# 64x64 score tiles and another order of steps in the attention stage of a two-layer trunk

## Chip, cores and metric

The kernel runs on one core of a Trainium2 chip. The metric is the device time of one execution in microseconds (us). Before the change the median of 3 runs is 2286.52 us (2284.51 to 2287.61).

## The reference

The program computes two residual layers of width 1024 over 1024 tokens in float32, and a final norm. The even layer mixes with retention and RWKV-7 heads, the odd layer with sliding-window attention, and a SwiGLU feed-forward net (FFN) follows each. The change lies in the attention of the odd layer: 16 query heads of 64 columns in 4 groups, one key and one value head to a group, a window of 128 tokens, and a learned sink value for each head that enters the softmax's maximum and its denominator.

```python
z = h @ w_qkv + b_qkv
q, k, v = jnp.split(z, [SWA_WIDTH, SWA_WIDTH + SWA_KV_HEADS * HEAD_DIM], axis=-1)
...
kb, vb = with_prev(k), with_prev(v)          # the block's own 128 keys, and the 128 before them
s = jnp.einsum('bnqhgd,bnkhd->bnhgqk', q, kb).astype(jnp.float32) * HEAD_DIM ** -0.5
...
band = (rel >= 0) & (rel < W)
...
m = jnp.maximum(jnp.max(s, axis=-1, keepdims=True), sink)
e = jnp.exp(s - m)
p = e / (jnp.sum(e, axis=-1, keepdims=True) + jnp.exp(sink - m))
o = jnp.einsum('bnhgqk,bnkhd->bnqhgd', p.astype(vb.dtype), vb)
return o.reshape(B, T, SWA_WIDTH) @ w_o + b_o
```

Each query sees 128 keys: from its own block those up to itself, and from the block before it the rest. So a square of 128 queries by 128 places holds all its scores: at each place stands either the own key or the previous block's key of the same number.

## The kernel before

**Halves and pairs.** The tokens are cut into two halves (hf 0 and 1) of 512. The attention stage works on 16 pairs, numbered 0 to 15: a pair is one half, one key group g and two neighbouring blocks of 128 queries, with the 4 heads of the group, so 8 squares of 128 by 128. Pairs 0 to 7 belong to half 0. Pairs 0, 2, 4 and 6 begin with the first block of the sequence, which has no block before it (k0 in the code).

**Four steps for each pair**, named by letters in ATTN_PLAN. S(j), `scores` and `block`: TensorE multiplies queries by keys into two PSUM tiles for each block (lines L1703; tags r and c for the pair's first block, m twice for the second). For each of the two heads i, there are two matmuls, e=1 and e=0, which stand in the two halves of TensorE's rows, since a head has 64 columns to contract over; each takes 128 queries and 256 keys (the form 64*128 64x256 in the trace). ScalarE copies the previous block's scores into the square s (L1712), VectorE overwrites it with the own scores where a constant mask allows (L1713). VectorE takes the maximum (L1728, L1729) and the sink term (L1730), ScalarE makes 8 exponentials with sums (L1733), VectorE and GpSimd multiply by the reciprocal (L1734, L1735, L1737), VectorE transposes 32 by 32 blocks into sq (L1743), and SyncE's queue sends sq to a DRAM tile pd. D(j), `fetch`: four DMAs on SyncE's queue bring pd back, rearranged, as pc (L1750). M(j), `sides`: VectorE multiplies pc by a mask (L1757), which keeps the own block's weights, and VectorE and GpSimd subtract the product from pc, each for 4 heads (L1760), which leaves those of the previous block; both are in pT. O(j), `out`: TensorE multiplies pT by the values into the PSUM tile y (L1773), ScalarE makes the high half of the result (L1779) and VectorE the low half (L1780), in the tile n that the output projection reads. Tile s has 1 buffer, sq 1, pc 2, pT 1; s and pc have 4 KB in each partition.

**Filling.** Between these steps ATTN_PLAN puts steps of other generators, a letter for one step: q and k project queries, keys and values of half 1 (function `proj`: 24 matmuls of 512 columns into a PSUM tile f at L1298, L1300 and L1301, then VectorE L1634 and ScalarE L1635), r is a norm, w is the output projection (w_o: `gemm`, L445, L447, L448), p and f are feed-forward work. In `kv` each of the two value projections is followed at once by four transposes on TensorE (L1665) of the projected tile nq into a PSUM tile m, and a ScalarE copy into vt. Weights are loaded by SyncE's queue (L400) into wr and split into a high part (ScalarE, L430) and a low part (VectorE or GpSimd, L431).

**What sets the order.** Each engine takes its instructions in one fixed order, and each wait holds up all behind it. A scheduler puts the instructions of VectorE, ScalarE, GpSimd and SyncE in order; ATTN_PLAN sets in which order they are handed to it, and `behind` ties one instruction behind another on the same engine. TensorE's order is written out in ATTN_ORDER, which `queue` applies: each entry a:n names PSUM tiles, numbered as they first appear, and takes n matmuls from them in turn. PSUM has three tiles f, two m, and one each of r, c and y.

Of the kernel before, what the change touches and what calls it, by code (L numbers as in the profile page):

```python
# [16 lines left out]
P = 128  # L17
# [35 lines left out]
def make_consts():  # L53
    c = np.zeros((P, NCO), np.float32)

    def put(name, v):
        o, w = CO[name]
        c[: v.shape[0], o : o + w] = v.reshape(v.shape[0], w)
# [39 lines left out]
    put("amask", np.concatenate([own, own.T], axis=1))  # L98
# [37 lines left out]
S0 qqq S1 qqq D0 S2 M0 qqk D1 S3 O0 M1 kkk D2 S4 O1 M2 kkk D3 S5 O2 M3 krr D4 S6 O3 M4 rrr D5 S7 O4 M5 rrr D6  # L136
S8 O5 M6 rr D7 S9 O6 M7 D8 S10 O7 M8 D9 wwwwwwww S11 D10 rr f rrrr S12 O8 M9 D11 p S13 O9 M10 D12 pp S14 O10 M11 D13 p
S15 O11 M12 D14 pp O12 M13 D15 p O13 M14 p O14 M15 p O15 p
"""
ATTN_ORDER = """  # L140
# [113 lines left out]
class Kern:  # L254
# [1355 lines left out]
    def attn_open(self, ap):  # L1610
        nc = self.nc
        m = self.const(ap, "amask").rearrange("p (m o t) -> p m o t", m=2, o=1)
        self.own = m[:, 0].to_broadcast([P, 2, P]).bitcast(mybir.dt.uint32)
# [23 lines left out]
    def kv(self, hf, nr, ap):  # L1637
# [20 lines left out]
        if hf:  # L1658
            G.tensor_copy(vt[:, 0, :], pvt[:, 4, :])
        for i in range(2):  # L1660
            vc = self.t(self.pp, [P, HT], "nq", 4)
            yield from self.proj(nr, 10 + i, vc, bias=self.col("bqkv", 10 + i))
            pt = self.pst("m", [P, 4, P])
# [15 lines left out]
    def attn(self, ap, outs, fill, plan):  # L1679
# [7 lines left out]
        ds, pcs, pTs, n8 = {}, {}, {}, {}  # L1687

        def block(hf, g, b, tags, s):
# [8 lines left out]
            pss = [self.pst(tags[e], [P, 2, 256]) for e in range(2)]  # L1698
# [10 lines left out]
            for e in range(2):  # L1709
                o = s.rearrange("p (i e) k -> p e i k", e=2)[:, e]  # L1710
                if not k0:
                    S.copy(o, pss[e][:, :, :P])  # L1712
# [346 lines left out]
```

## Time and profile before

| what | value |
|---|---|
| median of 3 runs | 2286.52 us |
| the profiled execution, its own time | 2286.15 us |
| span in its profile | 2284.4 us |
| instructions | 35190 |
| busy: PE, DVE, ACT, POOL | 2232.7, 1683.9, 1010.9, 1027.2 us |
| attention stage, by the trace | 1363 to 1650 us |

The columns and names: PE is TensorE, DVE VectorE, ACT ScalarE, POOL GpSimd, SP SyncE; a queue of an engine that issues DMAs has a q behind its name. In a list of the timeline each row has the start in us, the duration in us, the engine, the line in the code, the operation, output and inputs by the program's names, shapes, a count of merged instructions, and in brackets how long the engine had stood idle just before and what released it. In the table of stretches the columns are the stretch, its length, the busy time of each engine with its count of instructions, and PEclk, the clock that was granted to TensorE as a share of the full one. In the list of waits each row has an engine, its line and what it waited for, the sum in us, how often, and the longest wait. A busy TensorE is one that has matmuls in progress, not one at its peak.

### The profile page before, as it was taken

How to read it: one execution, taken by the hardware profiler on the slowest of the kernel's cores; microseconds unless marked ns; L12 is line 12 of the kernel's file. 1: busy time of each engine (PE TensorE's matmuls, PEld its weight loads, DVE VectorE, ACT ScalarE, POOL GpSimd, SP SyncE). 2: the span in 40 equal slices, each digit the busy share in tenths (PEclk: the TensorE clock that was granted, in tenths of full speed). 3: DMA queues.
4: the chain of work that ended last, by engine and by line, in shares of the span. 5: the costliest groups of instructions: out<-in, count | busy, mean ns of one | idle time of the engine just before them, and what ended most of it. 6: DMA issues, size and time to landing. Idle time of an engine off the chain costs nothing. (4 is left out here: it accounts for less than half of the span.)

```text
span 2284.4 us, 35190 instructions
## 1 busy us (share of the span) xinstructions
PE 2232.7 (98%) x12816; PEld 1789.4 (78%) x12816; DVE 1683.9 (74%) x2476; ACT 1010.9 (44%) x1906; POOL 1027.2 (45%) x800
## 2 busy tenths in 40 slices
PE   8999999999999999999999998999999999999998
PEld 6777777778878888888888886677688888888886
DVE  7877965876567368887895967877547788888866
ACT  5454544434445333333343465546444333343335
POOL 3122221212341167777777501214303677777675
PEclk9999999999999999999999999999999999999999
DMA  8566554444356456556766334444436466557663
GB/s 276 195 211 207 194 160 131 141 126 129 134 190 221 162 177 214 203 203 221 266 224 242 109 120 135 135 139 160 158 138 228 173 213 214 211 202 283 228 221 116
DMA packets 181853, 423.17 MB, mean 185 GB/s; under 512 B 44464, under 2 KB 55344, under 8 KB 181680
## 3 DMA queue, kind: packets, MB, share of 16 engines
q1 hardware_dynamic: 178272, 414.37, 53.0%
q10 hardware_dynamic: 2832, 4.45, 0.5%
q8 instruction: 102, 1.67, 0.3%
q0 software_dynamic: 576, 2.10, 0.2%
q14 instruction: 71, 0.58, 0.1%
HBM read 283.87 MB, written 131.60 MB: 182 GB/s over the span
## 5 line engine op out<-in xcount | busy, mean ns | idle before, releaser
L289 PE MATMUL ps_f<-n,w 128*128 128x512 f32 x1440 | 358.7, 403 | 8.6 <-ACT w L430 5.9
L289 PEld LDWEIGHTS ps_f<-n,w 128*128 128x128 f32 x1440 | 266.9, 189 | 83.2 <-issue 12.6
L431 POOL TENSOR_TENSOR w<-wr,w 128x512 fp32r<-128x512 f32 x63 | 87.8, 1401 | 296.4 <-ACT w L430 285.5
L430 ACT CAST w<-wr 128x512 fp32r<-128x512 f32 x231 | 140.6, 617 | 150.7 <-PE ps_f L448 50.3
L431 DVE TENSOR_TENSOR w<-wr,w 128x512 fp32r<-128x512 f32 x168 | 126.3, 755 | 61.9 <-ACT w L430 61.5
L1298 PE MATMUL ps_f<-n,w 128*128 128x512 f32 x415 | 166.4, 401 | 4.7 <-ACT u L1464 4.4
L1300 PE MATMUL ps_f<-n,w 128*128 128x512 f32 x415 | 163.7, 395 | 1.2 <-DVE n L462 1.2
L1301 PE MATMUL ps_f<-n,w 128*128 128x512 f32 x415 | 163.8, 395 | 0.0
L431 POOL TENSOR_TENSOR w<-wq,w 128x512 fp32r<-128x512 f32 x91 | 130.8, 1449 | 30.6 <-ACT w L430 30.6
L1298 PE MATMUL ps_m<-n,w 128*128 128x512 f32 x333 | 130.4, 392 | 0.0
L1300 PE MATMUL ps_m<-n,w 128*128 128x512 f32 x333 | 129.6, 389 | 0.0
L1301 PE MATMUL ps_m<-n,w 128*128 128x512 f32 x333 | 129.5, 389 | 0.0
L1308 DVE TENSOR_TENSOR nq<-ps_m,u 128x512 f32<-128x512 f32 x88 | 58.9, 684 | 93.9 <-PE ps_m L1301 93.9
L462 POOL TENSOR_TENSOR n<-nq,n 128x512 fp32r<-128x512 f32 x60 | 100.0, 1678 | 7.6 <-ACT n L460 7.6
L1493 POOL TENSOR_TENSOR w<-wd,w 128x512 fp32r<-128x512 f32 (+1 forms) x62 | 87.5, 1421 | 32.9 <-ACT w L1492 32.7
L1298 PEld LDWEIGHTS ps_f<-n,w 128*128 128x128 f32 x415 | 78.9, 190 | 27.6 <-ACT u L1464 5.2
L1300 PEld LDWEIGHTS ps_f<-n,w 128*128 128x128 f32 x415 | 78.9, 190 | 18.6 <-DVE n L462 1.6
L1301 PEld LDWEIGHTS ps_f<-n,w 128*128 128x128 f32 x415 | 78.7, 190 | 17.4 <-issue 0.7
L1298 PE MATMUL ps_m<-cb,w 128*128 128x512 f32 x236 | 91.9, 389 | 0.3 <-DVE nq L1308 0.3
L1300 PE MATMUL ps_m<-cb,w 128*128 128x512 f32 x236 | 91.8, 389 | 0.0
L1301 PE MATMUL ps_m<-cb,w 128*128 128x512 f32 x236 | 91.8, 389 | 0.0
L1493 POOL TENSOR_TENSOR w<-ws,w 128x512 fp32r<-128x512 f32 (+1 forms) x48 | 71.8, 1500 | 44.3 <-ACT w L1492 39.0
(533 smaller groups left out, 6355.8 us busy)
## 6 DMA issues: line engine op xcount, KB each, us to landing
hc<-n SPq DMA_DIRECT2D x84, 512.0 KB, 3.3
wsp<-w SPq DMA_DIRECT2D x54, 512.0 KB, 3.5
w<-wsp SPq DMA_DIRECT2D x54, 512.0 KB, 3.4
n<-hc SPq DMA_DIRECT2D x54, 512.0 KB, 6.7
wq<-in_w_gate SPq DMA_DIRECT2D x44, 512.0 KB, 4.4
u<-u SPq DMA_DIRECT2D x88, 256.0 KB, 3.2
ha<-hc SPq DMA_DIRECT2D x34, 512.0 KB, 5.6
hid<-n SPq DMA_DIRECT2D x66, 256.0 KB, 2.0
```

Of the source, the lines that this page charges most:

```text
L289: i = self.nc.tensor.matmul(out, lhsT, rhs, **kw)
L430: nc.scalar.copy(hi[:, :n], raw[:, c])
L431: self.lo.tensor_tensor(out=lo[:, :n], in0=raw[:, c], in1=hi.bitcast(F32)[:, :n], op=ALU.subtract)
L462: e.tensor_tensor(out=lo, in0=src, in1=hi.bitcast(F32), op=ALU.subtract)
L1298: i = mm(ps, hi, xh, start=first and k == 0, stop=False, skip_group_check=True)
L1300: mm(ps, hi, xl, start=False, stop=False, skip_group_check=True)
L1301: mm(ps, lo, xh, start=False, stop=last and k == len(w) - 1, skip_group_check=True)
L1308: self.last_add = V.tensor_tensor(out=o, in0=x, in1=y, op=ALU.add)
L1493: nc.gpsimd.tensor_tensor(out=lo, in0=v, in1=hi.bitcast(F32), op=ALU.subtract)
```

## The change

It has these parts.

1. Scores. A block's scores for one pair of heads come from 64x64 tiles of TensorE in place of two 64x128 ones: queries 0 to 63 take 192 keys (the previous block's 128 and the own block's first 64); queries 64 to 127 take the own block's 128 keys and the previous block's last 64, in two matmuls. For each i there are six matmuls, in the order 192 keys (e=1, e=0), 128 keys (e=1, e=0), 64 keys (e=1, e=0), in place of two; in the first block of the sequence there are four. The PSUM tile has 192 columns for each i in place of 256: columns 64 to 127 of the upper queries hold the previous block's keys, columns 0 to 63 and 128 to 191 the own ones. The mask for own keys is restricted to the query's own half of 64, and the overwriting (now L1732) reads the third group of 64 columns for both halves; in the first block ScalarE copies 64 columns for the upper 64 queries, 8 copies more in all.
2. s has 2 buffers, pc has 1.
3. The multiplication by the mask of M(j) (now L1779) stands behind the sink term's addition of S(j+2) (now L1752) on VectorE.
4. In `kv` both value projections come first, then the transposes (now L1670). In ATTN_PLAN the letters k are 10 in place of 8, and D(j) comes right after M(j-1).
5. ATTN_ORDER is written for the new tiles: the transposes of half 1 stand behind O5 and O6, and a third group of 18 output-projection matmuls stands ahead of O7.

```diff
--- before.py
+++ after.py
@@ -95,7 +95,8 @@
         g2[64:, p] = gm[2 * p + 1]
     put("gam", g2)
     own = np.tri(P, dtype=np.float32)
-    put("amask", np.concatenate([own, own.T], axis=1))
+    x = np.arange(P) // 64
+    put("amask", np.concatenate([np.where(x[:, None] == x[None, :], own, 0.0), own.T], axis=1))
     put("eps", np.tile(np.array([[RMS_EPS, RET_EPS, RWKV_EPS, math.log(0.5)]], np.float32), (P, 1)))
     return c
 
@@ -133,19 +134,19 @@
 
 
 ATTN_PLAN = """
-S0 qqq S1 qqq D0 S2 M0 qqk D1 S3 O0 M1 kkk D2 S4 O1 M2 kkk D3 S5 O2 M3 krr D4 S6 O3 M4 rrr D5 S7 O4 M5 rrr D6
-S8 O5 M6 rr D7 S9 O6 M7 D8 S10 O7 M8 D9 wwwwwwww S11 D10 rr f rrrr S12 O8 M9 D11 p S13 O9 M10 D12 pp S14 O10 M11 D13 p
-S15 O11 M12 D14 pp O12 M13 D15 p O13 M14 p O14 M15 p O15 p
+S0 qqq S1 qqq D0 S2 M0 D1 qqk S3 O0 M1 D2 kkk S4 O1 M2 D3 kkk S5 O2 M3 D4 krr S6 O3 M4 D5 rrr S7 O4 M5 D6 rrr
+S8 O5 M6 D7 krr S9 O6 M7 D8 k S10 O7 M8 D9 wwwwwwww S11 rr f rrrr S12 O8 M9 D10 p S13 O9 M10 D11 pp S14 O10 M11 D12 p
+S15 O11 M12 D13 pp O12 M13 D14 p O13 M14 D15 p O14 M15 p O15 p
 """
 ATTN_ORDER = """
-1:24 2:16 0:1 2:8 3:24 5:24 7:2 4:4 7:22 8:2 6:4 8:22 9:24 10:24 11:1 12,13:4 14,15:4 16:24 17:12 18,19:4 20,21:4
...
+1:24 2:16 0:1 2:8 3:24 4:24 7:22 5:4 7:2 8:2 6:4 8:22 9:24 10:24 11:1 12,13:8 14,15:12 16:24 17:12 18,19:12 20,21:12
...
 """
 
 
@@ -1610,7 +1611,7 @@
     def attn_open(self, ap):
         nc = self.nc
         m = self.const(ap, "amask").rearrange("p (m o t) -> p m o t", m=2, o=1)
-        self.own = m[:, 0].to_broadcast([P, 2, P]).bitcast(mybir.dt.uint32)
+        self.own = m[:, 0].rearrange("p o (x t) -> p o x t", x=2).to_broadcast([P, 2, 2, 64]).bitcast(mybir.dt.uint32)
         self.key = m[:, 1].rearrange("p o (q t) -> p q o t", q=4).to_broadcast([P, 4, 8, 32])
         self.sink = self.t(ap, [P, 16], "sink")
         nc.scalar.dma_start(self.sink, self.A["sinks"].to_broadcast([P, 16]))
@@ -1657,9 +1658,13 @@
             yield
         if hf:
             G.tensor_copy(vt[:, 0, :], pvt[:, 4, :])
+        vcs = []
         for i in range(2):
             vc = self.t(self.pp, [P, HT], "nq", 4)
             yield from self.proj(nr, 10 + i, vc, bias=self.col("bqkv", 10 + i))
+            vcs.append(vc)
+            yield
+        for i, vc in enumerate(vcs):
             pt = self.pst("m", [P, 4, P])
             for b in range(4):
                 nc.tensor.transpose(pt[:, b, :], vc[:, P * b : P * b + P], self.cst["ident"])
@@ -1684,7 +1689,7 @@
         mm = nc.tensor.matmul
         pairs = [(hf, g, b) for hf in range(2) for g in range(4) for b in (0, 2)]
         n = len(pairs)
-        ds, pcs, pTs, n8 = {}, {}, {}, {}
+        ds, pcs, pTs, n8, sinks = {}, {}, {}, {}, {}
 
         def block(hf, g, b, tags, s):
 
@@ -1695,26 +1700,43 @@
             k0 = int(hf == 0 and b == 0)
             k1 = P * b + P
             kp = k1 - P * (1 - k0)
-            pss = [self.pst(tags[e], [P, 2, 256]) for e in range(2)]
+            pss = [self.pst(tags[e], [P, 2, 192]) for e in range(2)]
+
+
             for i in range(2):
-                for e in (1, 0):
-                    a = slice(64 * e, 64 * e + 64)
-                    src = (kc if e == rg else ks)[ti]
-                    mm(
-                        pss[e][:, i, P * k0 :], qt[2 * g + i][a, P * b : P * b + P], src[a, kp : k1 + P],
-                        start=True, stop=True,
-                    )
+                parts = [(0, slice(kp, kp + 192), slice(0, 192))]
+                if k0:
+                    parts = [(0, slice(k1, k1 + 64), slice(P, 192))]
+                parts.insert(1, (1, slice(k1, k1 + P), None))
+                if not k0:
+                    parts.append((1, slice(kp + 64, kp + P), slice(64, P)))
+                for x, kk, c in parts:
+                    for e in (1, 0):
+                        a = slice(64 * e, 64 * e + 64)
+                        po = pss[e][64 * x : 64 * x + 64, i]
+                        r = (kc if e == rg else ks)[ti][a, kk]
+                        mm(
+                            po[:, c] if c else po.rearrange("p (y t) -> p y t", t=64)[:, 0:3:2],
+                            qt[2 * g + i][a, P * b + 64 * x : P * b + 64 * x + 64],
+                            r if c else r.rearrange("p (y t) -> p y t", t=64), start=True, stop=True,
+                            skip_group_check=True,
+                        )
             if k0:
                 G.memset(s, -1e30)
             for e in range(2):
                 o = s.rearrange("p (i e) k -> p e i k", e=2)[:, e]
-                if not k0:
+                if k0:
+                    S.copy(o[64:, :, :64], pss[e][64:, :, :64])
+                else:
                     S.copy(o, pss[e][:, :, :P])
-                V.copy_predicated(o, self.own, pss[e][:, :, P:])
+                V.copy_predicated(
+                    o.rearrange("p i (x t) -> p i x t", x=2), self.own,
+                    pss[e][:, :, P:].rearrange("p i (o t) -> p i o t", o=1).to_broadcast([P, 2, 2, 64]),
+                )
 
         def scores(j):
             hf, g, b0 = pairs[j]
-            s = self.t(ap, [P, 2, 4, P], "s", 1)
+            s = self.t(ap, [P, 2, 4, P], "s", 2)
             for i in range(2):
                 block(hf, g, b0 + i, ("rc", "mm")[i], s[:, i])
             s8 = s.rearrange("p b h k -> p (b h) k")
@@ -1727,7 +1749,7 @@
             m2, es2 = (t.rearrange("p (b h) -> p b h", b=2) for t in (m, es))
             V.tensor_reduce(out=m, in_=s8, axis=AX.X, op=ALU.max, negate=True)
             V.tensor_tensor(out=m2, in0=m2, in1=heads(self.nsink), op=ALU.min)
-            V.tensor_tensor(out=es2, in0=m2, in1=heads(self.sink), op=ALU.add)
+            sinks[j] = V.tensor_tensor(out=es2, in0=m2, in1=heads(self.sink), op=ALU.add)
             S.activation(es, es, AF.Exp)
             for h in range(8):
                 S.activation(s8[:, h], s8[:, h], AF.Exp, bias=m[:, h : h + 1], accum_out=den[:, h : h + 1])
@@ -1745,7 +1767,7 @@
             nc.sync.dma_start(d.rearrange("q t k x -> (q t) (k x)"), sq.rearrange("p k h t -> p (k h t)"))
 
         def fetch(j):
-            pc = pcs[j] = self.t(ap, [P, 4, 8, 32], "pc", 2)
+            pc = pcs[j] = self.t(ap, [P, 4, 8, 32], "pc", 1)
             for k in range(4):
                 nc.sync.dma_start(
                     pc[32 * k : 32 * k + 32].rearrange("p q h t -> p q (h t)"), ds[j][:, :, k].rearrange("q t x -> t q x")
@@ -1754,7 +1776,9 @@
         def sides(j):
             pc = pcs[j]
             pT = pTs[j] = self.t(ap, [P, 2, 4, 8, 32], "pT", 1)
-            V.tensor_tensor(out=pT[:, 1], in0=pc, in1=self.key, op=ALU.mult)
+            x = V.tensor_tensor(out=pT[:, 1], in0=pc, in1=self.key, op=ALU.mult)
+            if j + 2 in sinks:
+                self.behind(x, sinks[j + 2])
             for i, e in enumerate((V, G)):
                 h = slice(4 * i, 4 * i + 4)
                 e.tensor_tensor(out=pT[:, 0, :, h], in0=pc[:, :, h], in1=pT[:, 1, :, h], op=ALU.subtract)
```

Three places in the engines' orders. First VectorE, in the softmax of pair 4 (st holds its maxima, s its square; pT and pc belong to pair 2; n and ps_y to the output of pair 1; nq is a value projection). Before:

```order
L1728 TENSOR_REDUCE st_13202<-s_13182 128x8
L1757 TENSOR_TENSOR pT_13234<-pc_13177,c_amask_12331 128x1024
L1780 TENSOR_TENSOR n_2020_13102<-ps_y_13223,n_2016_13098 128x2x2x128
L1729 TENSOR_TENSOR st_13202<-st_13202,nsink_12335 128x8
L1760 TENSOR_TENSOR pT_13234<-pc_13177,pT_13234 128x4x128
L1730 TENSOR_TENSOR st_13202<-st_13202,sink_12333 128x8
L431 TENSOR_TENSOR w_13482<-wr_13480,w_13482 128x512
L1634 TENSOR_TENSOR nq_13239<-ps_f_13248,rs_12721 128x512
L1734 TENSOR_TENSOR st_13202<-st_13202 128x8
```

The same place of the changed kernel:

```order
L1750 TENSOR_REDUCE st_13276<-s_13242 128x8
L1751 TENSOR_TENSOR st_13276<-st_13276,nsink_12335 128x8
L1804 TENSOR_TENSOR n_2020_13162<-ps_y_13297,n_2016_13158 128x2x2x128
L1752 TENSOR_TENSOR st_13276<-st_13276,sink_12333 128x8
L1779 TENSOR_TENSOR pT_13308<-pc_13179,c_amask_12331 128x1024
L1784 TENSOR_TENSOR pT_13308<-pc_13179,pT_13308 128x4x128
L1756 TENSOR_TENSOR st_13276<-st_13276 128x8
```

The multiplication by the mask and the subtraction moved from between the maximum and the sink term to behind the sink term; the output's low half (L1780, now L1804) moved behind the first of the two small operations on the maxima, and the value projection moved out of this piece.

Second TensorE, at the transposes of the first value projection of half 1 (ps_f is a projection's PSUM tile, L1665 the four transposes, L1703 the scores of pair 5). Before:

```order
L1298 MATMUL ps_f_13290<-n_1944_12698,wx_13284 128x512
L1300 MATMUL ps_f_13290<-n_1948_12702,wx_13284 128x512
L1301 MATMUL ps_f_13290<-n_1944_12698,wx_13284 128x512
L1665 MATMUL ps_m_13275<-c_ident_154,nq_13239 128x128 x4
L1703 MATMUL ps_c_13310<-ks_1913_12469,q_1969_12795 128x256
L1703 MATMUL ps_r_13309<-kc_1908_12433,q_1969_12795 128x256
```

In the changed kernel the first transposes stand here, behind scores with their new tiles (L1718) and an output step (L1797):

```order
L1718 MATMUL ps_m_13778<-ks_2027_13198,q_2064_13466 64x2x64
L1718 MATMUL ps_m_13777<-kc_2004_13078,q_2064_13466 64x2x64
L1718 MATMUL ps_m_13778<-ks_2027_13198,q_2064_13466 64x64
L1718 MATMUL ps_m_13777<-kc_2004_13078,q_2064_13466 64x64
L1797 MATMUL ps_y_13816<-pT_13700,vt_12393 64x256 x8
L1670 MATMUL ps_m_13836<-c_ident_154,nq_13318 128x128 x4
L1299 MATMUL ps_f_13851<-n_1943_12697,w_13845 128x512
```

They moved from a place half a projection behind the one that they read, ahead of pair 5's scores, to one behind the output of pair 5.

Third TensorE, at the output of pair 7, the last of half 0 (n holds what the output projection reads; ps_f tiles are the output projection's). Before:

```order
L447 MATMUL ps_f_13912<-n_2022_13104,w_13909 128x512
L448 MATMUL ps_f_13912<-n_2018_13100,w_13909 128x512
L1773 MATMUL ps_y_13850<-pT_13799,vt_12393 64x256 x8
L1703 MATMUL ps_c_13810<-kc_2003_13029,q_2065_13383 128x256
L1703 MATMUL ps_r_13809<-ks_2026_13133,q_2065_13383 128x256
```

And in the changed kernel, where ps_f_14114 is the third output tile:

```order
L446 MATMUL ps_f_14114<-n_2018_13160,wx_14111 128x512
L448 MATMUL ps_f_14114<-n_2022_13164,wx_14111 128x512
L449 MATMUL ps_f_14114<-n_2018_13160,wx_14111 128x512
L1797 MATMUL ps_y_14018<-pT_13945,vt_12393 64x256 x8
L1718 MATMUL ps_c_13962<-kc_2004_13078,q_2064_13466 64x192
L1718 MATMUL ps_r_13961<-ks_2027_13198,q_2064_13466 64x192
```

In both orders the output of pair 7 is followed by the scores of pair 10, and those by the output projection's matmuls that read pair 7's result (6 for each tile held back). Two tiles stood ahead of it before and three now, 18 matmuls more.

14 rows, old and new, of the table ATTN_ORDER are left out of this document.

## Prediction

> **What bounds the kernel now.** I read the page first, then the stretches of the attention stage, then TensorE's waits in it, then the timelines around the longest waits.
>
> ```profile
> span 2284.4 us, 35190 instructions
> PE 2232.7 (98%) x12816; PEld 1789.4 (78%) x12816; DVE 1683.9 (74%) x2476; ACT 1010.9 (44%) x1906; POOL 1027.2 (45%) x800
> ```
>
> TensorE is busy for all but 51.7 us of the span. So only two things can shorten the program: TensorE standing idle less, and TensorE's work taking less time. The stretches of the attention stage, in the first three rows, show how much of either lies where the change is. The last four rows are short stretches in which the granted clock is half.
>
> ```profile
> 1363.00:1485.00 122.00, 108.24 (x581) 81.30 (x581) 94.61 (x157) 69.25 (x234) 22.71 (x18) 0.96 0.39 131
> 1485.00:1550.00 65.00, 60.39 (x272) 47.43 (x271) 45.88 (x76) 31.44 (x94) 11.05 (x8) 0.95 0.39 130
> 1550.00:1650.00 100.00, 93.28 (x476) 68.81 (x476) 63.64 (x93) 58.15 (x149) 41.05 (x29) 0.97 0.51 169
> 1425.30:1432.10 6.80, 3.05 (x14) 2.38 (x16) 5.20 (x8) 4.79 (x19) 1.46 (x1) 0.50 0.07 18
> 1442.40:1445.80 3.40, 3.16 (x10) 2.68 (x11) 3.39 (x4) 1.28 (x3) 1.58 (x2) 0.50 0.20 59
> 1500.40:1507.20 6.80, 5.65 (x13) 4.46 (x14) 6.10 (x11) 3.00 (x7) 1.27 (x1) 0.50 0.45 159
> 1609.60:1616.40 6.80, 5.60 (x13) 4.44 (x14) 4.95 (x10) 4.58 (x17) 4.21 (x3) 0.50 0.61 213
> ```
>
> TensorE is idle for 122 - 108.24 = 13.76 us, 65 - 60.39 = 4.61 us and 100 - 93.28 = 6.72 us: 25.1 us, half of the idle time of the whole span in an eighth of it. It also works 3.05 + 3.16 + 5.65 + 5.60 = 17.46 us at half clock, where the full clock would need half of that: another 8.7 us. Each of these stretches begins in or ends a long wait; here are TensorE's waits, with the sum, the count and the longest.
>
> ```profile
> PE ps_m L1665 <- ACT nq L1635: 10.3, 2, 7.8
> PE ps_f L1298 <- ACT u L1464: 4.8, 2, 4.4
> PE ps_f L447 <- DVE n L1780: 2.9, 1, 2.9
> PE ps_c L1703 <- DVE s L1713: 2.0, 1, 2.0
> PE ps_f L445 <- ACT n L1779: 1.8, 1, 1.8
> PE ps_y L1773 <- DVE pT L1760: 1.1, 3, 0.6
> PE ps_y L1773 <- DVE n L1780: 0.9, 1, 0.9
> ```
>
> The largest is the two transposes of half 1's values, which stand right behind the projections that they read, while VectorE and ScalarE evict these in turn behind a softmax. The output projection waits for pair 7's result (1.8 + 2.9). The others are a feed-forward wait (4.4), a score tile that is not yet free (2.0), and small ones.
>
> **The change part by part.**
>
> *Transposes of V.* They no longer stand ahead of pair 5's scores but behind outputs 5 and 6, a whole pair of work later, and the wait for L1635 (10.3) goes, with the half clock behind it: (3.05 + 3.16)/2 = 3.1. I keep 1 of it for a PSUM tile m that is now taken among scores. [...] In the trace the second of these waits lasted 10.3 - 7.8 = 2.5 us, and the clock stood at 0.50 for the 3.4 us from 1442.4 on, so a wait of 2.5 is priced with a half-clock stretch. [...]
>
> *The output of pair 7.* 18 more output-projection matmuls stand ahead of it. At a spacing of 0.23 us (the first two rows below) that is 4.1 us in which ScalarE gets through pair 9's exponentials, which stood in front of L1779. Waits of 1.8 + 2.9 and clock of 5.65/2 = 2.8 make 7.5; 0.5 stays.
>
> ```profile
> 1492.02 0.39 PE L447 MATMUL ps_f<-n,w 128*128 128x512 f32 x1
> 1492.25 0.39 PE L448 MATMUL ps_f<-n,w 128*128 128x512 f32 x1
> 1492.57 1.95 PE L1773 MATMUL ps_y<-pT,vt 128*64 128x256 f32 x16
> ```
>
> *Two buffers for s.* ScalarE's copies into s wait for the transpose out of the same buffer, and everything behind them on ScalarE waits too, u of the feed-forward net (L1464, 4.4) among it.
>
> ```profile
> ACT s L1712 <- DVE sq L1743: 23.4, 9, 4.6
> DVE st L1734 <- ACT s L1733: 12.3, 6, 2.5
> ```
>
> (The second row is VectorE's, for the first stretch alone, and is used below.) With a second buffer the first row's wait goes, so the score tiles come free earlier (2.0 of TensorE) and u is not held: 4.4 with its clock 5.60/2 = 2.8, of which I keep 1.0. VectorE's own order of copies is the same, so its part of the chain does not get shorter by this.
>
> *Masks later.* Between the maximum and the exponentials VectorE does other work, and then stands idle while ScalarE makes them:
>
> ```profile
> 1406.79 1.22 DVE L1728 TENSOR_REDUCE st<-s 128x8 f32<-128x1024 f32 x1
> 1407.93 1.22 DVE L1757 TENSOR_TENSOR pT<-pc,c_amask 128x1024 f32<-128x1024 f32 x1
> ...
> 1410.43 0.68 DVE L1760 TENSOR_TENSOR pT<-pc,pT 128x512 f32<-128x512 f32 x1
> ...
> 1413.86 0.17 DVE L1734 TENSOR_TENSOR st<-st 128x8 f32<-128x8 f32 x1 [2.07 <-ACT s L1733]
> 1414.91 1.53 DVE L431 TENSOR_TENSOR w<-wr,w 128x512 fp32r<-128x512 f32 x1
> 1420.77 1.22 DVE L1728 TENSOR_REDUCE st<-s 128x8 f32<-128x1024 f32 x1
> ```
>
> From one maximum to the next this chain took 1420.77 - 1406.79 = 13.98 us. L1757 (1.22) leaves the stretch ahead of the exponentials, and it and L1760 (0.68) now lie in the wait of 2.07, so the chain falls by 1.9 to 12.1 us. TensorE needs for a pair 36 projection matmuls (36 x 0.23 = 8.3), an output (1.95, the row above) and scores (1.93 before, 1.5 after, below): 11.7. The two are near each other. This pair's chain holds a split (L431) of 1.53 us, and without such a one TensorE leads; I allow the difference, 0.4 us, as a new wait in each of the eight pairs beside projections: 3.2. The two kinds of waits of L1773 (1.1 + 0.9) I let stay, since pT now comes later against its scores.
>
> *One buffer for pc.* Its next fetch starts after pair j's subtractions. The loop is the mask, GpSimd's subtraction, four issues on SyncE's queue (the median in ns is the middle number of the first row) and the landing (the last number of the third):
>
> ```profile
> L1750 SPq DMA_DIRECT2D pc<-pd x64: 303/428/507, 1382.0 to 1626.9; - x64
> L1760 POOL TENSOR_TENSOR pT<-pc,pT 128x512 f32<-128x512 f32 x16 | 21.5, 1345 | 73.6 <-DVE pT L1757 47.0 <-DVE st L1729 19.2 <-issue 5.4
> pc<-pd SPq DMA_DIRECT2D x64, 128.0 KB, 3.0
> SPq L400 <- DVE w L431: 52.7, 12, 8.1
> ```
>
> 1.2 + 1.35 + 4 x 0.43 + 3.0 = 7.3 us, below the 11.7 of a pair: I cost it at nothing, hidden behind TensorE's projections. The last row, waits of weight loads on that queue, is used in a rival below.
>
> *Scores.* One group of scores, and the output behind it, before; rows of the same group are left out:
>
> ```profile
> 1395.67 0.45 PE L1703 MATMUL ps_c<-kc,q 64*128 64x256 f32 x1 [1.98 <-DVE s L1713]
> 1395.68 0.48 PE L1703 MATMUL ps_r<-ks,q 64*128 64x256 f32 x1
> 1395.96 0.38 PE L1703 MATMUL ps_c<-kc,q 64*128 64x256 f32 x1
> ...
> 1396.18 0.38 PE L1703 MATMUL ps_c<-kc,q 64*128 64x256 f32 x1
> ...
> 1397.60 0.65 PE L1773 MATMUL ps_y<-pT,vt 128*64 128x256 f32 x4
> ```
>
> 16 rows in 1397.60 - 1395.67 = 1.93 us. A matmul leaves two rows (two passes of 256 columns), rows of the two tiles overlap, and one tile's passes come every 0.21 to 0.22 us (1395.96, 1396.18): 0.43 for each block and i. The new form does not occur in the trace; the nearest rows are 64x64 tiles elsewhere, and one form in two orders:
>
> ```profile
> 325.59 1.96 PE L289 MATMUL ps_m<-GG 64*64 64x128 f32 x32
> 80.18 1.15 PE L289 MATMUL ps_m<-c_ident,AR 64*64 64x64 f32 x32
> 225.36 1.71 PE L289 MATMUL ps_m<-AR,BK 64*128 64x128 f32 x16
> 534.74 1.17 PE L289 MATMUL ps_m<-AR,BK 64*128 64x128 f32 x16
> ```
>
> By the first two, two tiles at a time, a pass takes 1.96/16 = 0.12 us at 128 columns and 1.15/16 = 0.07 at 64, start and end of the burst included; by columns, 0.22/2 = 0.11 and 0.22/4 = 0.055. If all four tiles work at once, the lower queries' two passes of 192 columns (2 x 0.16) lie beside the upper queries' 2 x (0.11 + 0.055) = 0.33 to 2 x (0.12 + 0.07) = 0.38, and a block and i takes 0.33 in place of 0.43. There are 12 pairs with 4 of these and 4 with 2 (the sequence's first block reads 128 keys either way, at no gain): 56 x 0.095 = 5.3 us gained, or 2.8 by the longer end. If only two work at a time, it takes 2 x (0.16 + 0.11 + 0.055) = 0.65: 56 x 0.22 = 12.3 us lost. I take the gain: in the rows above the second tile's first pass (ps_r, 1395.68) starts ahead of the first tile's second pass (ps_c, 1395.96), though each matmul's two passes stand together in the program. So passes of tiles that share nothing overtake. The last two rows are the same 16 passes, 1.71 against 1.17 us, which shows that neighbours in program order matter. The 8 more copies on ScalarE, busy for 69.25 of the first stretch's 122 us, cost nothing.
>
> [...]
>
> *The sum.* Idle 25.1, clock 8.7, scores 5.3: 39.1 us at most. What stays: 1 at the transposes, 0.5 at output 7, 1.0 at u, 2.0 at L1773, 2.3 of the last stretch that no edit touches (6.72 - 4.44), and 3.2 of new waits: 10.0. The gain is 29. From the profiled execution's 2286.15 that gives 2257; it lies 0.4 below the median of the runs, which is nothing here.
>
> **The rivals.**
>
> *Two tiles at a time.* The upper queries' matmuls wait for the lower ones'. The score term turns from -5.3 to +12.3, 17.6 us more, of which about 4 hides the new waits: 2270. For it: no row shows four tiles at once. Against it: the overtaking of ps_r. Chance 0.12.
>
> *VectorE's chain becomes the bound.* In the first stretch VectorE is busy for 94.61 us; with its waits for ScalarE's exponentials (12.3 of its own waits there) it needs 106.9. TensorE would need 108.24 - 3.1 - 2.3 for scores (24 blocks and i) = 102.8, with some 6 of the allowances above on top. If copies, splits and evictions fall badly in its queue, as the split of 1.53 us did, a pair takes 13.1 in place of 12.1: 8 pairs x 1 us, and half of that in the second half, make 2269. Chance 0.16.
>
> *The waits stay under other names*, because they come of the order in which ScalarE and VectorE serve the softmax, not of where TensorE asks: 25 idle as before, scores a gain of some 3: 2283. Long waits fell on four places and the change moves each, so chance 0.04.
>
> *Slower: the fetch behind weight loads.* With one pc, D(j+1) can issue only after M(j), and SyncE's queue is in order. If a weight load (L400) that waits up to 8.1 us for its buffer stands ahead of the four issues, the loop is 7.3 + 8.1 = 15.4 us for a pair in place of 11.7. It decides from 11.7 - 7.3 = 4.4 us of waiting on. In 11 pairs that have projections or weights loaded beside them this makes 11 x 3.7 = 41 us, against 29 gained: 2298. For it: 12 such waits, 52.7 us in all. Against it: they are long because the loads run ahead, and a later load costs nothing. Chance 0.06.
>
> **How the numbers follow.** The forecast has the remaining 0.62, with 2246 to 2263 as its own range: the low end is new waits of nothing and 7 of the residues gone, the high end 2.5 less for scores and 3.5 more of waits. The first two rivals reach 2270 and carry 0.28; with 2.8 of scores either way and their own waits I go to 2276. Range 2245 to 2276; outside are the last two rivals (0.10) and the tails. A measurement of this kernel can tell about 0.2%, 4.6 us. Faster by more than that are the forecast and the first two rivals, 0.90; the third rival splits around the bound and is counted as same, 0.04; slower 0.06.
>
> **What would show it.** In the new profile: no wait of L1670 above 1 us, output-projection waits below 1, no half clock from 1363 to the end of attention, score groups that take about 1.5 us where they took 1.93, a period of about 12 us from one maximum to the next. The prediction is wrong if the score groups last above 2.5 us (two tiles at a time), if TensorE's waits name L1732, L1779 or L1784 again and again (VectorE's chain), or if L1779 waits for the DMA of pc (the fetch).

## The result, and the profile after

The changed kernel takes 2270.57 us (median of 4 runs, 2270.17 to 2271.66), the kernel before 2285.7 us in the same series: a ratio of 0.9935, 95% interval 0.9919 to 0.9951, so some 15 us faster. The forecast was 2257 in a range of 2245 to 2276. The side and the range hold; of the 29 us that were forecast half came.

Where the time went, by the trace. All times of the attention stage below are counted from its first score matmul, because the time at which that starts varies: it is 1363.2 us before and 1363.1 after, but from 1362.4 to 1368.5 in the profiles of the experiments, whose instructions ahead of it are the same. From there to the end of the last output the stage takes 1650.7 - 1363.2 = 287.5 us before and 1634.7 - 1363.1 = 271.6 after, 15.9 less; the spans differ by 16.0. All of the gain lies in the stage.

The three stretches of the stage in the changed kernel (columns as in the prediction: the stretch, its length, busy times of PE, PEld (TensorE's weight loads), DVE, ACT and POOL, then the clock), cut at about the same steps as in the prediction:

```profile
1363.00:1475.00 112.00, 103.40 (x867) 80.05 (x867) 98.83 (x165) 71.84 (x247) 24.89 (x19) 0.97 0.46 148
1475.00:1535.00 60.00, 60.00 (x350) 48.26 (x349) 41.67 (x68) 32.51 (x93) 9.78 (x7) 1.00 0.39 131
1535.00:1640.00 105.00, 94.78 (x618) 70.33 (x617) 69.15 (x98) 56.68 (x150) 39.99 (x29) 0.97 0.51 168
```

The output projection (second row) has no idle time left, where 4.6 us were. But TensorE is still idle for 8.6 us in the first and 10.2 us in the third stretch: 18.8 where 25.1 were. Its waits say where:

```profile
PE ps_f L1299 <- ACT u L1465: 8.1, 4, 6.5
PE ps_m L1670 <- DVE s L1732: 6.1, 2, 5.5
PE ps_y L1797 <- DVE pT L1784: 2.6, 4, 0.8
```

The transposes (now L1670) wait as before, under another name: not for their projection but for a PSUM tile m, which VectorE (L1732) has not yet read out after pair 8's scores. The feed-forward's u (now L1465) waits longer than before, 6.5 for 4.4. Each of the two waits is followed by half clock:

```profile
1462.40:1466.40 4.00, 4.00 (x12) 3.32 (x13) 3.90 (x7) 2.87 (x13) 0.24 (x1) 0.50 0.29 104
1597.70:1602.70 5.00, 4.98 (x12) 3.80 (x12) 1.90 (x2) 2.87 (x4) 4.00 (x3) 0.50 0.40 110
```

9 us of work at half clock, 4.5 lost, where 8.7 were. Idle time and clock together fell by 25.1 + 8.7 - 18.8 - 4.5 = 10.5 us; the other 5.4 of the 15.9 are what is left for the score work, by difference. The timeline of TensorE at pair 3's scores shows the tiles at work; the start of the group without the rows of ps_r, which stand up to 0.01 us behind those of ps_c, and without some of ps_c:

```profile
1392.61 0.37 PE L1718 MATMUL ps_c<-kc,q 64*64 64x192 f32 x1
...
1392.62 0.32 PE L1718 MATMUL ps_c<-kc,q 64*64 64x128 f32 x1
...
1392.78 0.27 PE L1718 MATMUL ps_c<-kc,q 64*64 64x128 f32 x1
...
1392.82 0.32 PE L1718 MATMUL ps_c<-kc,q 64*64 64x192 f32 x1
...
1392.89 0.22 PE L1718 MATMUL ps_c<-kc,q 64*64 64x64 f32 x1
...
1392.98 0.32 PE L1718 MATMUL ps_c<-kc,q 64*64 64x192 f32 x1
...
1393.31 0.32 PE L1718 MATMUL ps_m<-kc,q 64*64 64x192 f32 x1
```

The upper queries' 128 keys (1392.62) start 0.01 us behind the lower queries' 192 (1392.61), and the second pass of the 192 (1392.82) starts behind both passes of the 128, though it stands ahead of them in the program. So four tiles work at once. The first block and i takes 0.37 us, start of the group included (1392.61 to 1392.98), the one behind it 0.33 (to 1393.31), where 0.43 were; 0.33 to 0.38 was forecast.

What sets the pace is seen on VectorE. Here is its timeline from pair 4's maximum to pair 5's in the changed kernel:

```profile
1414.07 1.22 DVE L1750 TENSOR_REDUCE st<-s 128x8 f32<-128x1024 f32 x1
1415.33 0.17 DVE L1751 TENSOR_TENSOR st<-st,nsink 128x8 f32<-128x8 f32 x1
...
1416.09 1.22 DVE L1779 TENSOR_TENSOR pT<-pc,c_amask 128x1024 f32<-128x1024 f32 x1
1417.34 0.69 DVE L1784 TENSOR_TENSOR pT<-pc,pT 128x512 f32<-128x512 f32 x1
1418.91 0.27 DVE L1756 TENSOR_TENSOR st<-st 128x8 f32<-128x8 f32 x1 [0.88 <-ACT s L1755]
...
1420.06 1.53 DVE L432 TENSOR_TENSOR w<-wr,w 128x512 fp32r<-128x512 f32 x1
...
1423.27 1.25 DVE L432 TENSOR_TENSOR wx<-wr,wx 128x512 fp32r<-128x512 f32 x2
...
1425.91 1.22 DVE L1750 TENSOR_REDUCE st<-s 128x8 f32<-128x1024 f32 x1
```

The mask and the subtraction now lie in the wait for the exponentials, of which 0.88 us are left where 2.07 were. The period is 1425.91 - 1414.07 = 11.84 us, and VectorE is busy in all but that 0.88: it has no slack.

### The profile page after: what moved, and what is told of

It reads as the page before. It is cut to its first block, busy times and chain, and to the rows that moved or that the text cites. A ratio compares the mean times of both kernels' runs of the same rounds, so it can differ in the third digit from the quotient of the medians.

```text
span 2268.4 us, 36181 instructions
## 1 busy us (share of the span) xinstructions
PE 2222.8 (98%) x13296; PEld 1785.8 (79%) x13296; DVE 1687.9 (74%) x2476; ACT 1012.2 (45%) x1914; POOL 1024.7 (45%) x800
```

## The experiments

Three readings were to be told apart. A, that of the prediction: TensorE leads, and each long wait is a matter of the place where TensorE asks. B, the prediction's second rival: VectorE's chain from one maximum to the next sets the pace of the first ten pairs, and TensorE's waits are where its lead is given back. C, at one experiment: with work moved to GpSimd, GpSimd is the bound.

The table has all runs. "Nine periods" is the time from pair 0's maximum to pair 9's on VectorE, "stage" that from the first score to the end of the last output, both from the profiled execution. Ratios are to the kernel before on the same chip in the same series; it took 2285.7 us beside the changed kernel, 2286.91 beside e1 to e4, 2287.65 beside e5 to e8 and 2288.69 beside e9 to e12, so times of different series are compared by their ratios.

| kernel | us | ratio, 95% interval | nine periods | stage |
|---|---|---|---|---|
| before | 2285.7 | | 123.0 | 287.5 |
| changed | 2270.57 | 0.9935, 0.9919 to 0.9951 | 104.9 | 271.6 |
| e1 changed, old tiles | 2278.29 | 0.9959, 0.9944 to 0.9974 | 105.9 | 278.0 |
| e2 changed, u first | 2269.67 | 0.9917, 0.9901 to 0.9934 | 104.6 | 267.9 |
| e3 changed, first transposes earlier | 2270.14 | 0.9925, 0.9910 to 0.9939 | 104.5 | 270.8 |
| e4 e2 and e3 | 2269.93 | 0.9922, 0.9907 to 0.9936 | 104.5 | 267.8 |
| e5 changed, one s | 2270.62 | 0.9924, 0.9909 to 0.9939 | 104.7 | 270.1 |
| e6 changed, masks early | 2287.19 | 0.9999, 0.9990 to 1.0009 | 118.8 | 286.2 |
| e7 before, new tiles | 2287.57 | 0.9999, 0.9990 to 1.0009 | 123.6 | 289.4 |
| e8 changed, splits on GpSimd | 2260.97 | 0.9885, 0.9869 to 0.9902 | 93.5 | 260.2 |
| e9 e8 and u first | 2257.93 | 0.9870, 0.9853 to 0.9886 | 93.4 | 256.9 |
| e10 e8, old tiles | 2267.38 | 0.9908, 0.9893 to 0.9923 | 97.2 | 269.3 |
| e11 changed, two groups ahead of output 7 | 2272.52 | 0.9930, 0.9915 to 0.9944 | 104.9 | 271.5 |
| e12 before, masks later | 2272.61 | 0.9930, 0.9916 to 0.9945 | 109.9 | 271.3 |

### e3: the first transposes elsewhere

```diff
 ATTN_PLAN
-... S6 O3 M4 D5 rrr S7 O4 M5 D6 rrr
-S8 O5 M6 D7 krr S9 O6 M7 D8 k ...
+... S6 O3 M4 D5 rrr S7 O4 M5 D6 rrrk
+S8 O5 M6 D7 rr S9 O6 M7 D8 k ...
 ATTN_ORDER
-... 54:12 60:24 61,62:12 63,64:12 65:8
-66:4 67:24 ...
+... 54:12 60:12 61:4 60:12 62,63:12 64,65:12 66:8
+67:24 ...
```

Expected:

> The changed kernel with the first transposes of half 1's values in the middle of the last projection ahead of pair 8's scores, where both PSUM tiles m are free, in place of behind them. Theory A: the wait of 5.5 us is for a tile m that pair 8's scores hold until VectorE reads them; it goes, with 2.1 us of half clock: 2270.6 - 6 to 8 = 2263 to 2264. Rival B: VectorE's chain is 7 us behind TensorE there, so pair 9's scores or output 6 wait that much longer: 2269 to 2271.

Measured: 2270.14 us, no change. TensorE's waits in this kernel have these rows:

```profile
PE ps_f L1299 <- ACT u L1465: 8.2, 4, 6.5
PE ps_m L1718 <- ACT vt L1671: 3.2, 1, 3.2
PE ps_m L1670 <- DVE s L1732: 3.2, 1, 3.2
```

The wait of 5.5 us at the first transposes is gone, and two of 3.2 us stand at pair 8's scores and at the second transposes: 6.4 in place of 6.1. The nine periods are 104.5 us for 104.9. The place moved and the time did not, which is B.

### e2 and e4: u ahead of the last exponentials

```diff
-        self.nc.scalar.copy(u0, ps)
+        self.last_u = self.nc.scalar.copy(u0, ps)
...
-            S.activation(es, es, AF.Exp)
+            exps[j] = [S.activation(es, es, AF.Exp)]
...
+                if w == "pp" and 15 in exps:
+                    for x in exps.pop(15):
+                        self.behind(x, self.last_u)
```

Expected of e2, and of e4 with both edits:

> The changed kernel with pair 15's exponentials put behind the second copy of u on ScalarE. Theory A: the feed-forward wait of 6.5 us is ScalarE's order alone: u is ready at 1591.2 and stands behind exponentials that wait for VectorE until 1593.9. It goes, with 2.6 us of the half clock behind it: 2270.6 - 8 to 9 = 2262, and pair 15's chain doesn't start later. Rival B: the next step of the feed-forward work or output 12 waits for VectorE instead, and the time stays within 2 us of 2270.6.

> Both edits together, u ahead of the exponentials and the first transposes earlier. Theory A: the two add up, 2270.6 - 14 to 17 = 2254 to 2257. Rival B: 2267 to 2271.

The lines left out put the eight other exponentials into the same list. Measured: 2269.67 and 2269.93 us; their ratios cannot be told from the changed kernel's, and both times lie where B had them. In the trace of e2 u's wait of 6.5 is gone, and one for a later step of the same feed-forward pair (sg, L1355) is there, since that step now stands behind the exponentials:

```profile
PE ps_f L1299 <- ACT sg L1355: 2.4, 1, 2.4
PE ps_f L1299 <- ACT u L1465: 1.6, 3, 0.7
```

The stage is 3.7 us shorter (267.9), less than half of the 9 that wait and clock came to. By the trace, then, A was half right for the last pairs, and the rest went to the next wait on ScalarE's queue. That e4 is like e2 says again that the place of the transposes is worth nothing here.

### e6 and e12: the masks

e12 puts the tie into the kernel before, with nothing else; these are its lines, without the one that keeps the sink term's instruction in `sinks`. e6 takes the tie out of the changed kernel.

```diff
-            V.tensor_tensor(out=pT[:, 1], in0=pc, in1=self.key, op=ALU.mult)
+            x = V.tensor_tensor(out=pT[:, 1], in0=pc, in1=self.key, op=ALU.mult)
+            if j + 2 in sinks:
+                self.behind(x, sinks[j + 2])
```

Expected:

> The changed kernel without the tie of the mask multiplication to the sink term's addition, so that the masks may stand ahead of the exponentials again. Theory B: 1.2 to 1.9 us more on VectorE ahead of the exponentials in those pairs where the order puts them there, in some 5 to 7 of the first nine periods: periods of 13 to 14, 2270.6 + 7 to 12 = 2278 to 2283. Rival A (TensorE leads, VectorE has slack): periods stay at 12, 2270 to 2273.

> The kernel before with nothing but the tie of the mask multiplication behind the sink term's addition of two pairs later. Theory B: this edit carries nearly all of the gain, since it takes 1.2 us and more out of VectorE's chain ahead of the exponentials: periods of 12 to 13 in the first stretch, 2286.5 - 10 to 14 = 2272 to 2277. Rival A: the transposes still wait for their projections, 10 us with 3 of clock, and output 7 for its own: 2281 to 2286.

Measured: without the tie 2287.19 us, nothing left of the gain, though all other parts of the change are there; with the tie alone 2272.61 us, a ratio of 0.9930 against the 0.9935 of the whole change. The maxima of pairs 0 and 9 on VectorE, in e6 and then in e12:

```profile
1369.58 1.22 DVE L1750 TENSOR_REDUCE st<-s 128x8 f32<-128x1024 f32 x1
...
1488.41 1.21 DVE L1750 TENSOR_REDUCE st<-s 128x8 f32<-128x1024 f32 x1
```

```profile
1374.20 1.22 DVE L1728 TENSOR_REDUCE st<-s 128x8 f32<-128x1024 f32 x1
...
1484.07 1.22 DVE L1728 TENSOR_REDUCE st<-s 128x8 f32<-128x1024 f32 x1
```

118.83 us in the first and 109.87 in the second, 13.2 and 12.2 for a period. One wait makes 4 us of the difference. Without the tie pair 0's mask stands in pair 1's softmax, ahead of the reciprocal, and there it waits for its fetch, in the kernel before (first row) as in e6 (second):

```profile
1386.37 1.23 DVE L1757 TENSOR_TENSOR pT<-pc,c_amask 128x1024 f32<-128x1024 f32 x1 [4.04 <-DMA pc<-pd]
```

```profile
1386.76 1.23 DVE L1779 TENSOR_TENSOR pT<-pc,c_amask 128x1024 f32<-128x1024 f32 x1 [3.95 <-DMA pc<-pd]
```

In the changed kernel and in e12 VectorE waits for no fetch up to pair 9. B's expectation for e6 had only the masks' own 1.2 to 1.9 us in it, and the time came out 4 us above its range. TensorE's longest waits in the stage of e6, whose transposes stand in the new place, and of e12, whose transposes stand in the old one:

```profile
PE ps_m L1670 <- DVE s L1732: 10.7, 2, 7.9
PE ps_f L1299 <- ACT u L1465: 8.1, 4, 6.5
PE ps_y L1795 <- DVE n L1802: 5.4, 5, 1.6
```

```profile
PE ps_m L1665 <- ACT nq L1635: 6.0, 2, 5.5
PE ps_f L1298 <- ACT u L1464: 4.8, 2, 4.4
PE ps_y L1775 <- DVE pT L1762: 1.4, 3, 1.0
```

At the new place the transposes wait 10.7 us with early masks, about what they waited in the kernel before (10.3); at the old place they wait 6.0 with late masks, about what they wait in the changed kernel (6.1). The length of this wait follows VectorE's chain and not the place. The output projection's waits of 4.6 us are gone in both, so they too had two cures, and in e12 the masks alone are one.

e12 comes to the same sum by another way than the whole change. Its nine periods are 5.0 us longer than those of the changed kernel (109.9 for 104.9), and the rest of its stage is 5.3 shorter, where u's longest wait is 4.4 in place of 6.5. Which of the other parts makes the 5.0 us was not tried by itself.

### e5, e7 and e11: three parts that carry nothing here

```diff
 e5, in the changed kernel
-            s = self.t(ap, [P, 2, 4, P], "s", 2)
+            s = self.t(ap, [P, 2, 4, P], "s", 1)
 e11, in the changed kernel's ATTN_ORDER
-79:18 80:18 81:18 78:8 74,75:12 76,77:12 79:6 80:6 81:6
+79:18 80:18 78:8 74,75:12 76,77:12 79:6 80:6 81:24
```

e7 is the kernel before with the changed mask, `block` and the score entries of ATTN_ORDER alone. Expected:

> The changed kernel with one buffer for s again. Theory B (VectorE's softmax chain sets the pace from pair 0 to pair 9, 11.7 to 12.7 us from one maximum to the next): ScalarE's copies of a pair wait again for the transpose of the pair before, VectorE waits for them, and a period grows by some 0.5 to 1 us where nothing else lies between: 2270.6 + 4 to 9 = 2275 to 2280. Rival A (the second buffer only lets score tiles and u go earlier, TensorE's waits): 2 us or less in the first stretch, and the time stays at 2270 to 2273.

> The kernel before with the new score tiles alone. Theory B: its periods of 13.4 to 16.1 us stay, since VectorE sets them and the transposes' wait follows VectorE; the gain is that of the pairs behind the first stretch, 1 to 2 us: 2284 to 2286. Rival A: the tiles save their 5.3 us of TensorE's work: 2281.

> The changed kernel with the third group of 18 output-projection matmuls put back behind output 7, as before the change. Theory B: VectorE is late with pair 7's weights anyway, so output 7 comes no earlier and TensorE waits for it: 4 us of wait ahead of it or for its result, with a half clock of 1.5 to 3, part of which comes back: 2273 to 2276. Rival A: without the masks ahead of the chain the result is there in time: 2270 to 2272.

Measured: e5 2270.62 us, e7 2287.57 us, e11 2272.52 us. One buffer for s costs nothing, against what B was made to expect: the nine periods are 104.7 us, since VectorE's order has the transpose out of s ahead of the next pair's copies either way, and the copies on ScalarE fit between. It even takes 2.0 us off u's longest wait (4.5 for 6.5): on ScalarE both copies of u stand ahead of pair 15's exponentials again. The tiles alone give nothing to the kernel before: its nine periods stay (123.6 us), and the 1 to 2 us that B expected behind them did not come either, since the stage is 1.9 longer. e11 lies between its two ranges; its stage (271.5) and its three longest waits of TensorE (8.1, 6.1 and 2.6) are those of the changed kernel, as A has it. So the third group ahead of output 7 isn't needed once the masks are late.

### e8: VectorE relieved

```diff
         K.wx = ap, "wx", 2, False
-        K.lo = tc.nc.vector
+        K.lo = tc.nc.gpsimd
```

This moves the low parts of the weights from VectorE to GpSimd for the stage's first part. Expected:

> The changed kernel with the low parts of the weights of this stage's first projections (25.5 us of VectorE's 98.8 between 1363 and 1475) made by GpSimd, at about 1.4 us for each. Theory B: the periods fall from 12 to TensorE's 11.0 to 11.5, the transposes' wait of 5.5 us goes with its half clock: 2270.6 - 6 to 9 = 2262 to 2265. Rival A (the two waits are matters of place): VectorE gets idle and the time stays within 2 us. Rival C: GpSimd's multiplications of the softmax and its subtractions queue behind splits of 1.4 us each, and the chain gets no shorter: 2270 or above.

Measured: 2260.97 us, a ratio of 0.9885 (0.9869 to 0.9902), outside the interval of the changed kernel. The first stretch, then the waits of TensorE over the stage, all of them:

```profile
1363.00:1475.00 112.00, 111.88 (x916) 87.70 (x915) 84.00 (x147) 77.98 (x266) 64.50 (x50) 1.00 0.52 163
```

```profile
PE ps_f L1299 <- ACT u L1465: 8.2, 4, 6.5
PE ps_f L1301 <- DVE n L463: 1.3, 1, 1.3
PE ps_y L1797 <- DVE pT L1784: 0.5, 1, 0.5
```

VectorE is busy for 84.0 us in place of 98.8, GpSimd for 64.5 in place of 24.9, and TensorE is idle for 0.1 us of 112, without one wait for the transposes, which stand where they stood in the changed kernel. The nine periods are 93.5 us, 10.4 for each. TensorE had not waited for weights in the changed kernel either, so it is not their earlier arrival that helps. B is shown for the first ten pairs, with more gain than it expected, and C did not come: GpSimd has room.

### e1, e10 and e9: what a part is worth depends on who leads

e1 and e10 put the old `block`, mask and counts into the changed kernel and into e8; e9 puts e2's edit into e8. Expected:

> The changed kernel with the score tiles of before (two matmuls of 128 queries by 256 keys for a block and i) and everything else kept. Theory A: TensorE leads in the attention stage, and what the tiles save on it (5.3 us of work) shortens the program: 2270.6 + 5 = 2275 to 2276. Rival B: VectorE's softmax chain (a period of 11.7 to 12.7 us from one maximum to the next) sets the pace, and TensorE's shorter scores only become longer waits: 2270 to 2272, with the two long waits of the changed kernel (5.5 at the transposes, 6.5 at the feed-forward u) shorter by the same amount.

> The kernel of e8 with the old score tiles. In e8 TensorE waits for nothing above 0.3 us in the first ten pairs. Theory B: the tiles' saving on TensorE, hidden in the changed kernel, counts in full once TensorE leads: 3 us over the first nine pairs and 2 behind them, 2261.0 + 5 to 6 = 2266 to 2267, periods of the first stretch longer by 0.4 in full pairs. Rival: the chain is still the bound and the tiles are worth 1 us there: 2262 to 2263.

> The kernel of e8 (splits on GpSimd) with pair 15's exponentials put behind the second copy of u as well, as in e2. In e2 the last pair's output came 3.7 us earlier against the start of the stage than in the changed kernel. Theory B: the last pairs have no part of what e8 changed, so the same 3 to 4 us come off: 2261.0 - 3.5 = 2257 to 2258. Rival: now TensorE leads throughout, and the whole wait of 6.5 us with 2.6 of clock comes off: 2252.

Measured: e1 2278.29 us, e10 2267.38 us, e9 2257.93 us. Up to pair 9's maximum, counted from the first score, the old tiles cost 111.63 - 111.27 = 0.4 us in e1 and 102.95 - 99.85 = 3.1 us in e10. So while VectorE leads, TensorE's saving in the first stretch is worth next to nothing, as B has it, and it counts in full (3 expected) where TensorE leads. Over the whole stage they lose more, 278.0 - 271.6 = 6.4 us and 269.3 - 260.2 = 9.1, and e1 lies outside B's 2270 to 2272 and nearer to A's 2275 to 2276 (its interval overlaps that of the changed kernel by 0.0007). The rest isn't A's reason, though: it comes in the feed-forward part, where another wait appears with the old tiles, in e1 as in e10:

```profile
PE ps_f L1298 <- ACT sg L1354: 6.3, 1, 6.3
PE ps_f L1298 <- ACT u L1464: 3.5, 2, 3.2
```

It is a step that stands behind a pair's exponentials in ScalarE's order, as u did. The old tiles alone don't bring it, since in e12, which has them too, the wait for sg is 0.2 us. Why the order comes out so in e1 and e10 wasn't tried, so it stays open how much of the 8 us between e1 and the changed kernel is the price of the tiles. e9 is the fastest of all: 2257.93 us, 1.3% under the kernel before (0.9870, 0.9853 to 0.9886), as B expected; but its interval overlaps that of e8, and the gain of u shows in the stage alone (256.9 for 260.2).

## Why the prediction was right in sign and half in size

**Masks later.** The step that carries the gain. The prediction had the chain fall by 1.9 us a pair; it fell by (123.0 - 104.9)/9 = 2.0 on the mean. That the two agree so well is in part luck. The period that the prediction read fell from 13.98 to 12.21, by 1.8; but the one from pair 1 to pair 2 fell from 16.11 to 11.13, by 5.0, mostly by the wait of 4.04 us for a fetch, which the prediction does not have, and the other eight fell by 1.6 on the mean. All this was put down as what lets TensorE lead, and not summed; the sum was made of TensorE's waits. e12 shows that this one edit brings in the sum what the whole change brings, and e6 that the other parts bring nothing without it.

**The new waits of 3.2 us.** The step that failed first. The chain was set at 12.1 us and TensorE at 11.7, "0.4 us, as a new wait". The periods of the changed kernel come to 11.7 on the mean, near enough, but TensorE could have gone faster: once VectorE is relieved (e8) nine periods take 93.5 us, 10.4 each. The 11.7 had 36 projection matmuls and an output in every period, but the first three have no output step beside them yet, and the last has 24 projection matmuls. And a split of 1.53 us, without which TensorE was to lead, stands in every one of the nine periods of the changed kernel (1.46 in one of them), not in some. VectorE's chain costs 104.9 - 93.5 = 11.4 us, and the allowances for it (3.2, and 1 at the transposes) came to 4.2. The second rival, VectorE's chain as the bound at 2269, with a chance of 0.16, has what bounds these pairs. That its time lies so near 2270.57 is luck: it had pairs of 13.1 us, which came to 11.7, and no loss at u.

**Transposes of V.** The wait was taken to be of the place. It was to fall from 10.3 to 1 and fell to 6.1, with 2 us of half clock. e3, e6 and e12 show that its length follows the chain.

**Two buffers for s, and u.** The wait of u was to fall from 4.4 to 1.0. It rose to 6.5, with 2.5 of half clock: 8 us missed. The mechanism was wrong by one row of ScalarE's queue. With two buffers pair 15's copies do come earlier, but behind them, ahead of the second copy of u, stand the exponentials, and these wait for VectorE. On ScalarE in the changed kernel:

```profile
1593.91 0.40 ACT L1755 ACTIVATE s<-s,st 128x128 f32<-128x128 f32 x1 [5.24 <-DVE st L1751]
```

And TensorE's next matmul:

```profile
1597.72 0.79 PE L1299 MATMUL ps_f<-n,w 128*128 128x512 f32 x1 [6.47 <-ACT u L1465]
```

TensorE fell idle 6.47 us ahead of 1597.72, at 1591.25, with u's matmuls done, and the exponentials began only at 1593.91. e2 shows that the order was the cause of this wait, and that a later step takes over part of it; e5 shows that the second buffer brought this order.

**Output of pair 7.** No wait is left, as forecast, but e11 and e12 show that the third group of 18 is not needed for it.

**Scores.** Right in mechanism and size on TensorE: 0.10 us less for each block and i (0.33 for 0.43), where 0.095 was forecast. The passes do overtake, as was read from ps_r: those of the 128 keys start at 1392.62 and 1392.78, and the second one of the 192, which stands ahead of them in the program, at 1392.82. What was missed is that this is time only where TensorE leads (e7, e1, e10).

**One buffer for pc.** Costed at nothing, and no wait of TensorE names a fetch. But a sign that was given for the slow rival did come: VectorE's L1779 waits for the DMA of pc twice among the last pairs, 4.8 and 1.1 us. TensorE's waits for pT are 0.8 us at most, so little of it reaches TensorE. The part wasn't tried by itself.

Three more of the prediction's own signs spoke against it: L1670 waits 5.5 us where 1 was the limit, half clock comes twice in the stage, and TensorE's waits name L1732 and L1784, which was the sign of VectorE's chain. The two misses, 7.2 us by the chain (11.4 - 4.2) and 8 at u, are 15, against 13.6 between 2257 and 2270.57.

## What to carry to other kernels

A busy TensorE that waits at a few places may follow a slower engine: write down the period of that engine's chain from one step to the same step of the next tile, and that of TensorE without its waits, and compare them over the whole stretch before summing waits. Moving the place of a wait tests it cheaply: if the wait comes back elsewhere with the same sum, take work off the chain. And in an in-order queue, whoever frees an instruction from what stands ahead of it should read the next two rows as well, since one of them is what it waits for next.

## What the runs showed of the hardware

In these runs the length of a wait alone does not say what clock follows it. A wait of 1.98 us in the kernel before (at 1395.67, in the prediction) is followed by the full clock (1.00), one of 1.97 us in e7 by half clock (0.50), and one of 3.15 us in e3 by the full clock (1.00). The stretch behind the wait of the kernel before, then wait and stretch of e7, then those of e3:

```profile
1395.70:1398.50 2.80, 2.80 (x24) 2.19 (x26) 2.70 (x7) 0.84 (x5) 0.00 (x0) 1.00 0.86 275
```

```profile
1442.32 0.66 PE L1666 MATMUL ps_m<-c_ident,nq 128*128 128x128 f32 x4 [1.97 <-ACT nq L1636]
```

```profile
1443.30:1446.60 3.30, 3.30 (x9) 2.65 (x8) 2.98 (x3) 0.29 (x1) 1.30 (x2) 0.50 0.02 5
```

```profile
1474.43 0.66 PE L1670 MATMUL ps_m<-c_ident,nq 128*128 128x128 f32 x4 [3.15 <-DVE s L1732]
```

```profile
1474.40:1477.80 3.40, 3.37 (x17) 2.85 (x18) 3.32 (x6) 1.66 (x6) 0.00 (x0) 1.00 0.61 213
```

In the attention stage of the kernel before, half clock starts at 1425.30, 1442.37, 1500.40 and 1609.62, which is 5, 17 and 32 times 3.41 us from one to the next, and lasts 6.83, 3.41, 6.83 and 6.83 us. In the changed kernel it starts at 1459.76 and 1596.29, before the wait ends in both cases, and lasts 6.83 us each time. What decides whether half clock follows a wait was not shown. The wait of 1.98 us cost nothing beyond itself; that of 1.97 us cost half of the 3.30 us in its stretch, 1.65, on top.

And one split took 1.53 us at 1420.06 where two others took 1.25 together at 1423.27. GpSimd's timeline shows what ran beside the slow one:

```profile
1419.56 1.48 POOL L1759 TENSOR_TENSOR s<-s,st 128x512 f32<-128x512 f32 x1 [0.40 <-DVE st L1757]
```

The split began during GpSimd's multiplication, which ended at 1421.04, and ended itself 0.55 us later. All nine splits of 1.46 to 1.53 us between 1363 and 1475 in the changed kernel began during such a multiplication and ended 0.55 us behind it; the other 18, of 0.69 us at most, did not. No experiment moved the one against the other, so why these nine took longer was not shown.
